# Where two small jobs stand in a Hawk/FoX decoder step: the first decay rows, and one key page of two

## The chip, the cores and the metric

The kernel runs on one core of a Trainium2 chip. The metric is the device time of one execution in microseconds; of several executions the median counts.

## The reference

One layer of a hybrid decoder is computed for 512 prompt tokens and, with the same weights, for 8 sample sequences of one token each, which have 1024 cached tokens in pages of 128. Cut to what matters:

```python
z = h @ w_in                                   # h: normed, modulated x
xr, gr, q, k, v, fl, ga, gb = jnp.split(z, cuts, axis=-1)
ya = (rg_lru(conv(xr)) * jax.nn.gelu(gr)) @ w_proj_a          # branch A
logf = jax.nn.log_sigmoid(fl + b_f)            # one per token and head
# prompt, 16 heads of 64, per head:
s = q @ k.T * scale + Fq[:, None] - Fk[None]   # F: cumulated logf
o = softmax(where(causal, s, -inf)) @ v
# samples: the same over cache_k[page_table], cache_v[page_table], cache_logf
yb = o @ w_proj_b
x = x + g1 * ((sigmoid(ga) * ya + sigmoid(gb) * yb) @ w_o)
x = x + g2 * ((silu(gu) * up) @ w_ffn_out)     # gu, up = norm(x) @ w_ffn_in
```

## The kernel before

All activations are kept transposed, 1024 features as 8 tiles of 128 partitions by 520 tokens (512 and 8). Every product with a weight matrix is taken one column tile of 128 at a time, in two halves of 260 tokens. To keep float32 accuracy weights and activations are split in a high and a low part: ScalarE casts the weight tile (`whi`, L246), VectorE subtracts (`wlo`, L248), and TensorE runs three matmuls for each of the 8 rows of tiles (`part_product`, L305). A half is thus 24 matmuls.

The part that the change touches is the stage from about 300 to 490 us. It runs key product 0 (`k_product`), value product 0, branch A's eight products `pa0` to `pa7` (`branch_a`), and then a loop of eight steps `i` over pairs of heads. "Step 0" below is the turn `i = 0`. A step runs the key product of the next pair, the value product of the next pair, and in between the attention of this pair and the scores of the next. `k_product(i + 1, mid_a)` and `v_product(i + 1, mid_b)` call `mid_a` and `mid_b` between their two halves. Names on the way:

- `decay_rows(i)`: for each of two heads SyncE loads a row of cumulated forget values to all partitions (`fb`), and GpSimd makes the masked forms `f0`, `fm` and `fb` of it by one copy and four additions. `scores` adds them to the scores.
- `scores(i, blocks)`: TensorE makes `sc` from `ksA`, `ksB` (keys) and `qqA`, `qlA` and so on (queries); VectorE adds the decay and takes the minimum (`mu`); ScalarE takes the exponential; VectorE takes the reciprocal of the sums; ScalarE and GpSimd scale. Blocks 0 and 1 are done in `mid_b`, blocks 2 and 3 behind the value product.
- `turn`: TensorE transposes the probabilities (`ptt`), ScalarE and VectorE split them (`ph`, `pl`). `values` multiplies them with the values (`po`).
- the cached pages: 64 key pages and 64 value pages of 512 KB share seven buffers (`pg`). GpSimd's queue loads pages up to a point in the program, SyncE's queue the rest. `key_page` loads a key page and puts it on the list `pend`. `key_sum` multiplies a page with the sample's query (L730) and reduces it (L731, into `S`), both on VectorE; then the buffer is free for the next page. A value page is multiplied on TensorE (`pv`, L817) and frees its buffer thus. When all pages of two samples are summed, `past_softmax` runs a chain of small steps (L768 to L797: `lgt`, `st`, `mk`, `pw`).
- `at(i, part)` in the loop starts page loads and value products by two tables, `KEYS_AT` and `VALUES_AT`. Steps 0 to 2 load two key pages each at part 2, within `mid_b`. Two are pending when the loop starts.

A scheduler puts the program of each engine in order by priority, which follows the order of the calls; `tc.issue_after(x)` keeps an instruction behind another in that order. Buffers in one heap (`slot`) rotate, so that the order of the calls also sets which buffer a tile gets. Every engine and every queue works in its order, and a DMA that waits holds up what is behind it in its queue.

Of the kernel before, what the change touches and what calls it, by code (L numbers as in the profile page):

```python
# [65 lines left out]
def kernel(ctx, tc, xT, par, gates, b_f, cst, cse, own, cache_k, cache_v, cache_lf, pt,  # L66
# [3 lines left out]
    pe, act, dve, pool, sp = nc.tensor, nc.scalar, nc.vector, nc.gpsimd, nc.sync  # L70
# [9 lines left out]
    def slot(name, cols=NT, dt=F32, parts=128):  # L80
        return heap.tile([parts, cols], dt, name=name, tag="slot")

    def bank(name, parts=128, cols=512):
        return psp.tile([parts, cols], F32, name=name, tag="bank")

    def small(name, parts, cols, bufs=4):
        return sm.tile([parts, cols], F32, name=name, tag="s_" + name, bufs=bufs)
# [71 lines left out]
    for jt in range(FF // 128):  # L159
# [5 lines left out]
        for name in BLOCKS:  # L165
            units.append((c, name, 4))
            if name in JOIN[jt]:
                g, i = JOIN[jt][name]
# [12 lines left out]
    state = {"n": 0, "dma": 0, "split": 0, "load": 22, "lead": 11, "due": 0, "age": 1}  # L181
    stores = []

    def store(dst, src):
        stores.append((dst, src))
# [4 lines left out]
    def flush():  # L190
        while stores:
            sp.dma_start(*stores.pop(0))
# [125 lines left out]
    def product(name, a, evac, mid=None):  # L318
        n = begin()
        for j in range(2):  # L320
            b = bank(f"{name}_{j}")
            half_product(n, j, a, b)
            evac(j, b[:, :HALF])
            if j == 0 and mid is not None:
                mid()
        run_later(n)

    def to(t, fn):
        def evac(j, b):
            t0, t1 = HALVES[j]  # L330
            fn(t[:, t0:t1], b)
        return evac
# [270 lines left out]
    ftd = drp.tile([H, NP], F32, name="ftd")  # L603
# [82 lines left out]
    pend = []  # L686
# [32 lines left out]
    def key_sum():  # L719
        _, s, j, pg, q, half = pend.pop(0)  # L720
        r = s // 2
        c = 256 * (r % 2) + 32 * j + H * (s % 2)
        with tc.issue_after(state["last"].ins):
            if half is not None:
                b, c = 8 * (r % 2) + j, H * (s % 2) + 8 * half
                dve.tensor_tensor(pg, pg, q.unsqueeze(1).to_broadcast([128, 2, 512]), ALU.mult)
                dve.tensor_reduce(S[r // 2].rearrange("p (b c) -> p b c", c=32)[:, b:b + 2, c:c + 8],
                                  pg.rearrange("p j (h d) -> p j h d", d=DH), AX.X, ALU.add)
            else:
                dve.tensor_tensor(pg, pg, q, ALU.mult)  # L730
                last = dve.tensor_reduce(S[r // 2][:, c:c + H], pg.rearrange("p (h d) -> p h d", d=DH), AX.X, ALU.add)  # L731
        summed[r] += 1
        if summed[r] == 2 * NPAGE:
            chains.append([9, past_softmax(r)])
        return None if half is not None else last
# [307 lines left out]
    def branch_a(i, mid=None):  # L1043
        product(f"pa{i}", g, to(tA[i], lambda t, b: dve.tensor_tensor(t, b, t, ALU.mult)), mid)
        store(tAd[i], tA[i])
# [93 lines left out]
    def q_load(i):  # L1139
        kvs[i]["qr"] = slot("qA", NP), slot("qB", NP)  # L1140
        for a, pr in enumerate(HEADS):
            for to_ in HEADS:
                sp.dma_start(kvs[i]["qr"][a][to_], qd[i, pr, :NP])

    def q_split(i):
        qq = slot("qqA", NP, F32R), slot("qqB", NP, F32R)
        ql = slot("qlA", NP, F32R), slot("qlB", NP, F32R)
        for a in range(2):
            t = kvs[i]["qr"][a]
            act.activation(qq[a], t, AF.Copy, scale=-(DH ** -0.5))  # L1150
            state["last"] = dve.scalar_tensor_tensor(ql[a], t, -(DH ** -0.5), qq[a].bitcast(F32), ALU.mult, ALU.subtract)
        del kvs[i]["qr"]
        kvs[i]["q"] = qq, ql

    def v_product(i, mid=None):
        t = slot("vt")
        product(f"v{i}", h, to(t, act.copy), mid)
        kvs[i]["vt"] = t
        pool.tensor_copy(v8[:, NS * i:NS * i + NS], t[:, NP:])
        store_now(vT[128 * i:128 * i + 128, :], t)  # L1160
# [17 lines left out]

    def decay_rows(i):
        for hd in (2 * i, 2 * i + 1):
            a = hd % 2
            if a == 0:
                f0 = slot("f0", 256)
            fb = slot("fb", 512)
            sp.dma_start(fb, ftd[hd:hd + 1, :].partition_broadcast(128))
            fm = slot("fm", 512)
            pool.tensor_copy(fm[:, :256], fb[:, :256])
            for dst, b in ((f0[:, 128 * a:128 * a + 128], 0), (fm[:, 384:], 1), (fm[:, 256:384], 2), (fb[:, 384:], 3)):  # L1190
                pool.tensor_tensor(dst, fb[:, 128 * b:128 * b + 128], msk, ALU.add)
            fmb = fm.rearrange("p (b c) -> p b c", b=4)
            fbs[hd] = f0[:, 128 * a:128 * a + 128], fmb[:, 0::3], fm[:, :384], fb

    def scores(i, blocks):
        ks = kvs[i]["k"]
        qq, ql = kvs[i]["q"]
        mus = small("mu", 128, 12, 4).rearrange("p (c b a) -> p c b a", c=3, b=2)
        for b in blocks:
            n = 128 * b  # L1200
            for a, pr in enumerate(HEADS):
                hd = 2 * i + a
                if b == 0:
                    prob[hd] = []
                    t3 = slot("p3", 512), slot("p02", 512), slot("p1", 256)
                    pts[hd] = (t3[1][:, :128], t3[2], t3[1][:, 128:], t3[0])
                sc = bank(f"sc{hd}_{b}")
                pe.matmul(sc[:, :n + 128], lhsT=qq[a][:, n:n + 128], rhs=ks[a][:, :n + 128], start=True, stop=False)
                pe.matmul(sc[:, :n + 128], lhsT=ql[a][:, n:n + 128], rhs=ks[a][:, :n + 128], start=False, stop=True)
                p = pts[hd][b]  # L1210
                mu = mus[:, :, b - blocks[0], a]
                ins = p[:, :n + 128], sc[:, :n + 128]
                if b == 1:
                    ins = [t.rearrange("p (b c) -> p b c", b=2) for t in ins]
                dve.tensor_tensor_reduce(ins[0], fbs[hd][b], ins[1], 1.0, 3.0e38, ALU.add, ALU.min, mu[:, 0:1])  # L1215
                act.activation(p[:, :n + 128], p[:, :n + 128], AF.Exp, bias=mu[:, 0:1], scale=-1.0, accum_out=mu[:, 1:2])  # L1216
                prob[hd].append((p, mu))
        dve.reciprocal(mus[:, 2], mus[:, 1])  # L1218
        for b in blocks:
            for a in range(2):  # L1220
                p, mu = prob[2 * i + a][b]
                (pool.tensor_scalar(p, p, mu[:, 2:3], None, ALU.mult) if a and i + 1 < KT else act.activation(p, p, AF.Copy, scale=mu[:, 2:3]))  # L1222
# [102 lines left out]

    k_product(0)
    q_load(0)
    decay_rows(0)
    v_product(0)
    for i in range(KT):  # L1330
        branch_a(i, (lambda: scores(0, (0, 1))) if i == KT - 1 else None)
        if i == 4:
            q_split(0)
            q_load(1)
    scores(0, (2, 3))
    g = None
    state.update(load=14, lead=8)
# [3 lines left out]
    def at(i, part):  # L1341
        tick(KEYS_AT[i][part], VALUES_AT[i][part])
        flush()

    for i in range(KT):
        last = i + 1 == KT

        def mid_a():
            v_tokens(i)
            if last:  # L1350
                turn(i, 0)
            at(i, 0)
            if last:
                with in_place():
                    join_weights()

        def mid_b():
            if not last:
                turn(i, 1)
            if not last:  # L1360
                scores(i + 1, (0, 1))
            at(i, 2)

        if not last:
            q_split(i + 1)
            decay_rows(i + 1)
        keys = None
        while pend:
            keys = key_sum()
            after[state["split"] + 2] = keys  # L1370
        if last:
            gate_b(6, mid_a)
        else:
            k_product(i + 1, mid_a, keys)
        turn(i, 1 if last else 0)
        at(i, 1)
        if i + 2 < KT:
            q_load(i + 2)
        (gate_b if last else v_product)(7 if last else i + 1, mid_b)
        values(i)  # L1380
        if last:
            spread_weights()
        if not last:
            scores(i + 1, (2, 3))
            at(i, 3)
        else:
            some_values(32)
        if i == KT - 4:
            sp.dma_start(em, cse)
        if i == KT - 2:  # L1390
            merge_load(0)
            state.update(load=22, lead=11)
# [344 lines left out]
```

## Time and profile before

| what | value |
|---|---|
| median of 3 runs | 1028.36 us (1027.15 to 1031.1) |
| profiled execution | 1033.71 us |
| its span | 1032.1 us |
| TensorE busy | 997.7 us, 97% of the span |
| VectorE busy | 793.5 us, 77% |
| ScalarE busy | 552.5 us, 54% |
| GpSimd busy | 330.7 us, 32% |
| HBM, read and written | 192.49 and 13.09 MB |

In the rows of the profile PE is TensorE, DVE VectorE, ACT ScalarE, POOL GpSimd and SP SyncE. In a timeline a row gives the start, the duration, the engine, the line, the operation, and output and input tiles; the bracket says how long the engine had been idle before it and what ended that. "PE pv L817 <- DMA pg" in the waits reads: TensorE's instruction that writes `pv` on line 817 waited for the load of a page. In the windows PEclk is the granted TensorE clock as a share of full speed, and the DMA share is that of the 16 engines' time.

### The profile page before, as it was taken

The page shows a single profiled execution, that of the slowest core. Times are in us where ns is not written, and L with a number is a line of the kernel's source. Part 1 is how long each engine was busy: PE and PEld are TensorE (multiplying, and loading weights), DVE is VectorE, ACT ScalarE, POOL GpSimd, SP SyncE. Part 2 cuts the span into 40 slices and gives each one's busy share as a digit, 9 for nine tenths or more (in the row PEclk, how much of TensorE's full clock was granted, in tenths as well). Part 3 has the DMA queues.
Part 4 walks back from the last instruction along what each step waited for, and adds up shares of the span by engine and source line. Part 5 has one row for each costly group of instructions (what it writes and reads, how often), then busy time and mean ns, then how long its engine had stood idle before and what let it go on. Part 6 is the DMA issues. An engine that isn't in the chain of part 4 may idle for free.

```text
span 1032.1 us, 21298 instructions
## 1 busy us (share of the span) xinstructions
PE 997.7 (97%) x7994; PEld 922.1 (89%) x7994; DVE 793.5 (77%) x1423; ACT 552.5 (54%) x1132; POOL 330.7 (32%) x424
## 2 busy tenths in 40 slices
PE   4999999999999999999999999999999999999996
PEld 1888989999898988878888989999999999999996
DVE  5446999998999977886756544778878888888864
ACT  4433665857682266776876223555444444445453
POOL 0214511111135134554430001485433423424212
PEclk9899999999999999999999999999999999999998
DMA  9888987878898998999665784323343342333212
GB/s 330 298 270 290 306 288 210 274 230 274 260 272 297 340 322 254 295 283 275 197 240 183 251 304 139 83 62 100 86 123 88 98 124 65 99 104 102 62 63 83
DMA packets 164378, 206.98 MB, mean 201 GB/s; under 512 B 9890, under 2 KB 125106, under 8 KB 164210
## 3 DMA queue, kind: packets, MB, share of 16 engines
q1 hardware_dynamic: 147554, 152.52, 47.7%
q0 software_dynamic: 13040, 46.67, 13.8%
q10 hardware_dynamic: 3680, 6.42, 1.7%
q8 instruction: 63, 1.03, 0.4%
q14 instruction: 41, 0.34, 0.1%
HBM read 192.49 MB, written 13.09 MB: 199 GB/s over the span
## 4 chain that ended last, share of the span: by engine, by line
PE 77%; DVE 10%; DMA 5%; ACT 4%; issue 3%; POOL 1%; SPq 0%; POOLq 0%; DVEq 0%; ACTq 0%
PE fo L305 12%; PE pb L305 4%; PE gb L305 4%; PE k L305 4%; PE v L305 3%; PE ga L305 3%; PE pa L305 3%; PE wo L305 3%; PE pv L817 2%; PE gr L305 2%; PE xr L305 2%; DMA wraw<-in_w_in_dram 2%; PE qp L527 2%; PE po L1265 2%; PE q L527 1%
## 5 line engine op out<-in xcount | busy, mean ns | idle before, releaser
L246 ACT CAST whi<-wraw 128x1024 fp32r<-128x1024 f32 (+1 forms) x79 | 82.1, 1040 | 135.2 <-PE pb L305 35.3
L248 DVE TENSOR_TENSOR wlo<-wraw,whi 128x1024 fp32r<-128x1024 f32 (+1 forms) x79 | 100.1, 1268 | 31.3 <-ACT whi L246 29.2
L270 ACT CAST wb<-ws 128x512 fp32r<-128x512 f32 x72 | 44.8, 622 | 92.2 <-PE fo L305 64.4
L305 PE MATMUL fo<-ach,wb 128*128 128x260 f32 x512 | 93.2, 282 | 0.0
L682 POOL DMA_DIRECT2D pg<-in_cache_k_dram x74 | 39.4, 533 | 141.8 <-DVE S L731 76.1
L305 PEld LDWEIGHTS fo<-ach,wb 128*128 128x128 f32 x512 | 78.9, 188 | 0.0
L271 DVE TENSOR_TENSOR wb<-wraw,wb 128x512 fp32r<-128x512 f32 x86 | 74.0, 860 | 6.0 <-ACT wb L270 5.0
L261 POOL TENSOR_TENSOR ws<-wraw 128x512 f32<-128x512 f32 x18 | 26.7, 1485 | 153.7 <-DMA wraw<-in_w_fi_dram 135.1
L270 ACT CAST wb<-wraw 128x512 fp32r<-128x512 f32 x86 | 53.4, 621 | 37.1 <-ACT cp L1625 6.2
L305 PE MATMUL fo<-acl,wb 128*128 128x260 f32 x256 | 72.3, 282 | 0.0
L271 DVE TENSOR_TENSOR wb<-ws,wb 128x512 fp32r<-128x512 f32 x72 | 59.9, 832 | 15.1 <-ACT wb L270 13.3
L730 DVE TENSOR_TENSOR pg<-pg,qb 128x1024 f32<-128x1024 f32 x48 | 58.4, 1236 | 1.3 <-DMA pg<-in_cache_k_dram 1.2
L731 DVE TENSOR_REDUCE S<-pg 128x16 f32<-128x1024 f32 x48 | 57.1, 1210 | 0.1
L1222 POOL TENSOR_SCALAR p<-p,mu 128x128 f32<-128x128 f32 (+3 forms) x28 | 35.6, 1282 | 51.6 <-DVE mu L1218 39.6
L305 PEld LDWEIGHTS fo<-acl,wb 128*128 128x128 f32 x256 | 48.2, 188 | 0.0
L1216 ACT ACTIVATE p<-p,mu 128x128 f32<-128x128 f32 (+3 forms) x64 | 35.3, 553 | 13.6 <-DVE mu L1215 13.3
L305 PE MATMUL v<-hh,whi 128*128 128x260 f32 x128 | 37.9, 296 | 0.6 <-DVE pl L1236 0.3
L305 PE MATMUL pb<-oh,whi 128*128 128x260 f32 x128 | 36.9, 288 | 1.0 <-ACT oh L1323 1.0
L305 PE MATMUL k<-hh,whi 128*128 128x260 f32 x128 | 37.3, 292 | 0.0
L817 PE MATMUL pv<-pg,pw 128*32 128x512 f32 x256 | 35.1, 604 | 2.0 <-DMA pg<-in_cache_v_dram 1.8
L305 PE MATMUL ga<-hh,wlo 128*128 128x260 f32 x128 | 36.3, 284 | 0.8 <-DVE wlo L248 0.8
L305 PE MATMUL gb<-hh,whi 128*128 128x260 f32 x128 | 37.0, 289 | 0.0
(1099 smaller groups left out, 3980.6 us busy)
## 6 DMA issues: line engine op xcount, KB each, us to landing
araw<-in_ada_w_dram SPq DMA_DIRECT2D x48, 512.0 KB, 6.9
wraw<-in_w_fi_dram SPq DMA_DIRECT2D x44, 512.0 KB, 4.1
pg<-in_cache_k_dram POOLq DMA_DIRECT2D x42, 512.0 KB, 6.2
pg<-in_cache_v_dram SPq DMA_DIRECT2D x42, 512.0 KB, 5.2
wraw<-in_w_in_dram SPq DMA_DIRECT2D x34, 512.0 KB, 7.3
wraw<-in_w_in_dram SPq DMA_DIRECT2D x11, 1024.0 KB, 10.4
pg<-in_cache_v_dram POOLq DMA_DIRECT2D x22, 512.0 KB, 6.6
pg<-in_cache_k_dram POOLq DMA_DIRECT2D x32, 256.0 KB, 5.9
```

Of the source, the lines that this page charges most:

```text
L246: state["act"] = act.copy(hi[:, :k1 - k0], src)
L248: state["last"] = dve.tensor_tensor(lo[:, :k1 - k0], src, hi[:, :k1 - k0].bitcast(F32), ALU.subtract)
L270: state["act"] = act.copy(t[:, :4], src)
L271: state["last"] = dve.tensor_tensor(t[:, 4:], src, t[:, :4].bitcast(F32), ALU.subtract)
L305: state["mm"] = pe.matmul(out[:, :t1 - t0], lhsT=wt[k], rhs=at, start=k == 0 and m == 0, stop=k == nk - 1 and m == 2)
L527: state["mm"] = pe.matmul(b[:, :HALF], lhsT=wt, rhs=at[:, t0:t1], start=k == 0 and m == 0, stop=k == 3 and m == 2)
L682: done.append(eng.dma_start(pg, cache[bass.ds(r, 1), :, c0:c1].rearrange("a p c -> (a p) c")))
L730: dve.tensor_tensor(pg, pg, q, ALU.mult)
L731: last = dve.tensor_reduce(S[r // 2][:, c:c + H], pg.rearrange("p (h d) -> p h d", d=DH), AX.X, ALU.add)
L817: pe.matmul(pv[0][32 * gq:32 * gq + 32, :], lhsT=pw[r][:, c:c + 32], rhs=pgs[gq // 2][:, 512 * hf:512 * hf + 512], start=j == 0, stop=j == ...
L1216: act.activation(p[:, :n + 128], p[:, :n + 128], AF.Exp, bias=mu[:, 0:1], scale=-1.0, accum_out=mu[:, 1:2])
L1222: (pool.tensor_scalar(p, p, mu[:, 2:3], None, ALU.mult) if a and i + 1 < KT else act.activation(p, p, AF.Copy, scale=mu[:, 2:3]))
```

## The change

Two jobs are put elsewhere; the number of instructions on each engine stays.

```diff
+    decay_raw = {}
+
+    def decay_load(i):
+        for hd in (2 * i, 2 * i + 1):
+            decay_raw[hd] = slot("fb", 512)
+            sp.dma_start(decay_raw[hd], ftd[hd:hd + 1, :].partition_broadcast(128))
+
     def decay_rows(i):
+        if 2 * i not in decay_raw:
+            decay_load(i)
         for hd in (2 * i, 2 * i + 1):
             a = hd % 2
             if a == 0:
                 f0 = slot("f0", 256)
-            fb = slot("fb", 512)
-            sp.dma_start(fb, ftd[hd:hd + 1, :].partition_broadcast(128))
+            fb = decay_raw.pop(hd)
             fm = slot("fm", 512)
...
-        dve.reciprocal(mus[:, 2], mus[:, 1])
+        state["sums"] = dve.reciprocal(mus[:, 2], mus[:, 1])
...
     k_product(0)
     q_load(0)
-    decay_rows(0)
+    decay_load(0)
     v_product(0)
     for i in range(KT):
+        if i == 2:
+            decay_rows(0)
         branch_a(i, (lambda: scores(0, (0, 1))) if i == KT - 1 else None)
...
             if not last:
                 scores(i + 1, (0, 1))
+            while pend:
+                with tc.issue_after(state["sums"].ins):
+                    key_sum()
             at(i, 2)
...
         keys = None
-        while pend:
+        if pend:
             keys = key_sum()
             after[state["split"] + 2] = keys
```

The GpSimd work of the first pair's decay rows is called before `pa2`; its two loads stay where they were. For every pair both loads now come ahead of the GpSimd work. Of the pending key pages only one is summed ahead of the key product of a step, the rest in `mid_b`, behind the reciprocal of the scores and ahead of the next page loads.

GpSimd between key product 0 and the pages that it loads, before (`qk` belongs to the key product, `v` to the value product):

```order
L1136 TENSOR_TENSOR qk_4420<-kt,q_573 128x8
L1189 COPY fm<-fb 128x256
L1191 TENSOR_TENSOR f_4516<-fb,cs 128x128
L1191 TENSOR_TENSOR fm<-fb,cs 128x128 x2
L1191 TENSOR_TENSOR fb<-fb,cs 128x128
L682 ISA
L682 DMA pg<-in_cache_k_dram 128x1024
```

and now:

```order
L1136 TENSOR_TENSOR qk_4420<-kt,q_573 128x8
L1159 COPY v_4421<-vt 128x8
L1199 TENSOR_TENSOR fb<-fb,cs 128x128
L682 ISA
L682 DMA pg<-in_cache_k_dram 128x1024
L682 ISA
L682 DMA pg<-in_cache_k_dram 128x1024
L682 ISA
L682 DMA pg<-in_cache_v_dram 128x1024
```

Before, the second head's five operations and the copy of `v` stood between these key pages and the first value pages. Now one addition of the ten operations is ahead of the pages; the nine others stand behind two more key pages.

VectorE in step 1, from the queries' split to the keys' split, before:

```order
L1151 SCALAR_TENSOR_TENSOR qlB<-qB,qqB 128x512
L730 TENSOR_TENSOR pg<-pg,qb 128x1024 x2
L731 TENSOR_REDUCE S<-pg 128x16 x2
L248 TENSOR_TENSOR wlo<-wraw,whi 128x1024
L1131 TENSOR_TENSOR ksA<-k_0_5816,ksA 64x260
```

and now, with the second page's place behind the reciprocal in two pieces:

```order
L1151 SCALAR_TENSOR_TENSOR qlB<-qB,qqB 128x512
L730 TENSOR_TENSOR pg<-pg,qb 128x1024
L731 TENSOR_REDUCE S<-pg 128x16
L1131 TENSOR_TENSOR ksA<-k_0_5814,ksA 64x260
L1131 TENSOR_TENSOR ksB<-k_0_5814,ksB 64x260
```

```order
L1226 RECIPROCAL mu<-mu 128x4
L730 TENSOR_TENSOR pg<-pg,qb 128x1024
L248 TENSOR_TENSOR wlo<-wraw,whi 128x1024
L731 TENSOR_REDUCE S<-pg 128x16
L1223 ISA p_6023,mu<-fm,sc_2_6134 128x384
```

One page's two operations have left the stretch ahead of `ksA` and stand ahead of the second half of the scores; `wlo` of the value product, which was ahead of `ksA`, follows the two key splits. In step 0 the second page likewise stands right behind the reciprocal. In step 3 the chain of the last two samples' softmax (L768, L770) starts half a step later.

SyncE's queue in step 1, around the pair's second value page (`pg_6178`), before:

```order
202 L682 DMA pg_6167<-in_cache_v_dram 128x1024 [waits DMAHW5_49,DMAHW4_49,PE_49]
203 L1143 DMA qA_5959<-qd_572 64x512 [waits DMAHW6_49]
204 L1143 DMA qA_5959<-qd_572 64x512 [waits DMAHW7_49]
205 L1143 DMA qB_5960<-qd_572 64x512 [waits DMAHW0_49]
206 L1143 DMA qB_5960<-qd_572 64x512 [waits DMAHW1_49]
207 L681 TENSOR_LOAD ptb_103
208 L681 ISA x2
209 L682 ISA
210 L682 DMA pg_6178<-in_cache_v_dram 128x1024 [waits DMAHW2_49,PE_49]
```

and now:

```order
213 L681 TENSOR_LOAD ptb_103
214 L681 ISA x2
215 L210 DMA wraw_6631<-in_w_in_dram 128x8x128 [waits DMAHW2_49,DVE_49]
216 L210 DMA wraw_6631<-in_w_in_dram 128x8x128 [waits DMAHW4_49]
217 L682 ISA
218 L682 DMA pg_6178<-in_cache_v_dram 128x1024 [waits DMAHW5_49,DVE_49]
219 L682 ISA
220 L682 DMA pg_6272<-in_cache_v_dram 128x1024 [waits DMAHW6_49,PE_49]
```

It waited for TensorE and stood ahead of the weights; now it waits for VectorE, for the sum of the second key page, whose buffer it gets, and stands behind them.

## The prediction

> **What bounds the kernel now.** I read the profile's page first, then TensorE's waits in the stage that the change touches, and then the chain and the timelines at the longest of them. The page:
>
> ```profile
> span 1032.1 us, 21298 instructions
> PE 997.7 (97%) x7994; PEld 922.1 (89%) x7994; DVE 793.5 (77%) x1423; ACT 552.5 (54%) x1132; POOL 330.7 (32%) x424
> ```
>
> TensorE is busy for 97% of the span and the change gives it the same matmuls. Time can only come from its idle stretches or from its clock. TensorE's waits between 295 and 565 us (total, times, longest):
>
> ```profile
> PE pv L817 <- DMA pg<-in_cache_v_dram: 1.8, 1, 1.8
> PE ptt L1231 <- ACT ph L1235: 1.3, 2, 0.7
> PE ptt L1231 <- DVE ksB L1131: 0.7, 1, 0.7
> PE sc L1208 <- DVE pl L1236: 0.6, 4, 0.2
> ```
>
> One wait is for a value page; the others lie where the transposed probabilities (`ptt`) and scores (`sc`) wait for VectorE or for ScalarE behind it. Busy time and granted clock of TensorE in the four places, and in the stretch behind the second:
>
> ```profile
> core 0: us, PE busy (x), PEclk, DMA share, GB/s
> 330.00:333.00 3.00, 1.16 (x11) 1.00 0.99 386
> 381.00:386.60 5.60, 3.60 (x26) 1.00 0.98 363
> 455.00:460.00 5.00, 3.83 (x28) 1.00 1.04 370
> 480.00:484.30 4.30, 4.04 (x33) 1.00 0.92 307
> 386.80:390.30 3.50, 3.50 (x18) 0.51 0.98 178
> ```
>
> Idle: 1.84 us in branch A's product, 2.00 in step 0, 1.17 in step 3, 0.26 in step 4. Each restart costs a little more. In the first place matmul starts stand 2.12 us apart (rows below) where pa's stand 0.12 apart: 2.00 lost for 1.84 idle, so 0.16 per restart. With about five restarts in step 0, four in step 3 and two in step 4 (my count of the stops) the losses are an estimated 2.8, 1.8 and 0.6 us. The last row is the price behind step 0: the clock is halved for 3.5 us.
>
> **Part 1, GpSimd's decay rows.** GpSimd, ScalarE and TensorE before pa3 (branch A's fourth product), and the loads' time to landing between 300 and 340 us (the last row):
>
> ```profile
> 317.12 0.40 POOL L1189 COPY fm<-fb 128x256 f32<-128x256 f32 x1 [5.67 <-DMA fb<-ftd]
> 322.10 1.09 POOL L682 DMA_DIRECT2D pg<-in_cache_k_dram  x2
> 325.58 0.18 POOL L1159 COPY v<-vt 128x8 f32<-128x8 f32 x1
> 325.71 1.08 POOL L682 DMA_DIRECT2D pg<-in_cache_v_dram  x2
> 318.32 1.05 ACT L246 CAST whi<-wraw 128x1024 fp32r<-128x1024 f32 x1 [4.70 <-PE pa L305]
> 330.70 0.28 PE L305 MATMUL pa<-gl,whi 128*128 128x260 f32 x1
> 332.82 2.25 PE L817 MATMUL pv<-pg,pw 128*32 128x512 f32 x8 [1.84 <-DMA pg<-in_cache_v_dram]
> pg<-in_cache_v_dram POOLq DMA_DIRECT2D x4, 512.0 KB, 7.5
> ```
>
> The value pages are issued at 325.71 because all ten decay operations and the wait for fb (5.67 us, to 317.12) stand ahead; they land about 7 us later (median 7.5), and `pv` stands until 332.82. In the new order one decay addition stays ahead, which still waits for fb (to about 317.1), then two key and two value pages. Four issues of 0.54 us put the value pages at about 318.6 to 319.3; a free buffer may hold them a little. Landing is at about 326.8, 4 us before the product before them ends at 330.8. The wait goes whole, **-2.0 us**. Two moved things cost nothing: the nine other decay operations run behind the page issues, and their readers are scores(0), behind pa's last product; the copy of v is ahead of the pages now but waits only for ScalarE, which has 4.70 us of idle time there.
>
> **Part 2, step 0.** The chain there:
>
> ```profile
> 375.08 2.35 DVE pg L730 x2
> 377.43 0.07 DVE S L731
> 378.48 1.21 DVE S L731
> 379.69 0.53 DVE mk L791
> 380.22 1.14 DVE wlo L248
> 381.38 0.42 DVE ksA L1131
> 386.57 4.66 PE v L305 x24
> ```
>
> Two multiplications and two reductions stand ahead of `ksA`. One pair of them moves behind the reciprocal: 1.17 + 1.21, say **2.35 us** earlier. VectorE has room for it there:
>
> ```profile
> 393.71 0.68 DVE L1269 TENSOR_TENSOR ol<-po,oh 64x512 fp32r<-64x512 f32 x1 [4.36 <-ACT side L1268]
> ```
>
> 4.36 us of idle time hold 2.35 us. But this chain is released by loads, and the DMA engines are at 0.92 to 1.04 of their time in every window above. If the load doesn't move up with the 2.0 us of part 1, TensorE arrives earlier at a chain that doesn't. I take half: 2.35 - 1.0 = **-1.35 us**, with bounds of -0.35 (no move) and -2.35 (all of it). Left of the stall: 2.8 - 1.35 = 1.45 us.
>
> **The clock.** The 24 matmuls behind step 0 take 4.66 us; a like group in step 1:
>
> ```profile
> 411.42 2.98 PE v L305 x24
> ```
>
> The difference is 1.68 us. The windows above tell when: after a loss of 2.8 us in 5.6 the clock halved; after 1.8 us in 5 and after one gap of 2.0 it stayed at 1.00. With 1.45 us left I take it as not halving: **-1.7 us**; bounds 0 and -1.7. [...]
>
> **Part 3, steps 3 and 4.** Step 3's chain:
>
> ```profile
> 450.56 1.05 ACT whi L246
> 451.64 1.43 DVE wlo L248
> 453.07 0.89 DVE S L768 x2
> 453.98 0.63 DVE mk L770
> 454.62 0.42 DVE ksA L1131
> ```
>
> The softmax rows at L768 and L770 move half a step later, behind the scores, and one page goes too. What is late next is `wlo`, which waits for `whi`: `ksA` starts at 453.1, not 454.62, **-1.5 us** of 1.8. In step 4 the reduction `mk` (0.53 in step 0) leaves the chain: **-0.5 us**. The moved rows' results are needed a step later and more; should their cover fail, TensorE would pay at most the same 1.5.
>
> **Part 4, what the change adds.** In steps 1 and 2 the page sum stands behind the reciprocal, and the pair's second value page waits for its buffer. Step 1 now:
>
> ```profile
> 414.55 0.18 DVE L1218 RECIPROCAL mu<-mu 128x4 f32<-128x4 f32 x1 [1.04 <-ACT p L1216]
> 415.79 1.23 DVE L248 TENSOR_TENSOR wlo<-wraw,whi 128x1024 fp32r<-128x1024 f32 x1 [1.07 <-ACT whi L246]
> 423.05 1.06 PE L817 MATMUL pv<-pg,pw 128*32 128x512 f32 x8
> pg<-in_cache_v_dram SPq DMA_DIRECT2D x42, 512.0 KB, 5.2
> DMA to landing us min/median/max: 3.4/5.3/9.0
> ```
>
> From 414.73: multiplication 1.2, `wlo` 1.2, reduction 1.2, so the page is issued at about 418.4. Its `pv` is the second half of the row at 423.05, about 423.6: 5.2 us, against a median of 5.2 and a spread of 3.4 to 9.0 between 385 and 470 us. No wait for these pages is among TensorE's waits of before. Taken: 0.3 us in each of steps 1 and 2, **+0.6**; bounds 0 and 3.8 each. Step 0 has some 4 us more, since `wlo` is late there. Queued behind that wait on SyncE are the next value pages, which wait for `pv` anyway; q's rows and the weights go ahead. In steps 1 and 2 `wlo` and the second half of the scores are at most 1.3 us late (2.4 of work against 1.07 of idle time); no row of TensorE's waits names those probabilities, so they have slack now: 0, bound 1.3 each.
>
> GpSimd scales probabilities beside the moved multiplication:
>
> ```profile
> 422.91 4.67 POOL L1222 TENSOR_SCALAR p<-p,mu 128x384 f32<-128x384 f32 x2 [1.07 <-DVE mu L1218]
> ```
>
> Two of them take 4.67 us while VectorE multiplies. [...]
>
> **Sum.** -2.0 - 1.35 - 1.7 - 1.5 - 0.5 + 0.6 = **-6.45 us**. The profiled execution took 1033.71 us (span 1032.1 and 1.6 around it), 5.35 above the median of 1028.36; the terms are stalls of the same stages, so I subtract from both: 1027.3 there, and a median of **1021.9**.
>
> **Rivals.**
> 1. *Value pages become the wait (slower).* The page of each of steps 1, 2 and 3 lands late. For: it is issued in the last moment, and the maximum is 9.0. Against: the median. Being slower by over 0.5% (5.1 us) needs 5.1 + 6.45 + 0.6 = 12.2 us from three places, 4.1 each: 2.4 of waiting and one halved clock of 1.7. So it decides from a landing of 5.2 + 2.4 = 7.6 us on; at 9.0 it is 3 x (3.8 + 1.7) = 16.5 - 7.05 = +9.4, 1037.8 us. Chance 0.17.
> 2. *The clock drop stays*, being tied to something else than these stalls: -4.75, 1023.6 us. For: step 3 and the gap of 1.84 us had no drop. Against: it is the only one in the stage and stands right behind its worst place. Chance 0.14.
> 3. *The loads set step 0.* Nothing of part 1 is passed on: step 0 gives -0.35, 2.45 us of stall remain, and the clock halves: -2.0 - 0.35 - 1.5 - 0.5 + 0.6 = -3.75, 1024.6 us. For: DMA near 1.0. Chance 0.10.
> 4. *It does not do what it says*: loads, which set the pace of the stage, fill each gap that it clears: 0, 1028.4 us. For: the DMA shares. Against: each of the four places names another releaser. Chance 0.07.
>
> **How the numbers follow.** The forecast has 0.52. Its own range: -8.1 (all of step 0, no page wait) to -5.1, 1020.3 to 1023.3. A measurement tells 0.5% (5.1 us: 1023.2 and 1033.5) from no change. Faster: 0.50 of the forecast and a third of rival 2, 0.55. Slower: rival 1 and some scatter, 0.19. The rest, 0.26, is the same. The range leaves out rival 1 and the ends: from 1020.3 less 1.2 of scatter (1028.36 - 1027.15) to rival 4 and about 1.2 above, **1019.1 to 1029.6**.
>
> **What would show it.** Right: no `pv` wait within pa; the value pages issued near 319 us; `ksA` of step 0 with one `pg` and one `S` ahead; PEclk at 1.00 behind it; `ksA` of step 3 right behind `wlo`. Wrong: `pv` rows with a releaser in_cache_v in steps 1 to 3, a stall in step 0 of over 2 us, or a halved clock in a new place.

## The result and the profile after

The changed kernel takes 1026.15 us (median; 1022.38 to 1030.44) against 1029.12 us (1027.15 to 1032.38) of the kernel before beside it. The ratio is 0.9961, with a 95% interval of 0.9947 to 0.9974: some 4 us less (2.7 to 5.5; the two medians alone differ by 3.0). The median is inside the predicted range of 1019.1 to 1029.6 us, but the gain is under two thirds of the predicted 6.45 us, and by the text's own bound of 0.5% it is "the same", to which the prediction gave 0.26.

The page after, the same two lines as before:

```profile
span 1025.3 us, 21277 instructions
PE 994.1 (97%) x7994; PEld 921.1 (90%) x7994; DVE 792.7 (77%) x1423; ACT 553.3 (54%) x1132; POOL 331.4 (32%) x424
```

TensorE's waits in the stage (total, times, longest), all that there are:

```profile
PE pb L305 <- ACT oh L1331: 1.0, 1, 1.0
PE ptt L1239 <- ACT ph L1243: 0.7, 1, 0.7
PE v L305 <- ACT row L797: 0.5, 2, 0.3
PE sc L1216 <- DVE pl L1244: 0.5, 3, 0.2
PE v L305 <- DVE pl L1244: 0.3, 1, 0.3
```

The `pv` row of before is gone, and so is one of the two `ptt` waits on `ph` and nearly all of the one on `ksB`. The rows of `pb` (1.0) and `v` (0.3 and 0.3) stood in the profile of before too, where the prediction's list leaves them out; one wait of `v` for `row` is new. GpSimd and TensorE in branch A:

```profile
315.05 0.46 POOL L1199 TENSOR_TENSOR fb<-fb,cs 128x128 f32<-128x128 f32 x1 [1.46 <-DMA fb<-ftd]
315.69 1.20 POOL L682 DMA_DIRECT2D pg<-in_cache_k_dram  x2 [0.17 <-issue]
317.66 1.18 POOL L682 DMA_DIRECT2D pg<-in_cache_v_dram  x2 [0.78 <-PE pv L817]
329.00 1.07 PE L817 MATMUL pv<-pg,pw 128*32 128x512 f32 x8
```

One addition is ahead of the pages, the value pages go out 8.0 us earlier (the stage itself starts 1.9 us earlier, a matter of the program's start, see the end), held by a buffer for 0.78 us, and `pv` takes 1.07 us where it took 2.25. That shorter row is worth 1.1 us more, which the prediction had in its fence and did not read: the second page of the pair landed later still, and TensorE waited for it within the row (3.1 us in all).

Step 0 on ScalarE and VectorE:

```profile
368.82 0.63 ACT L1150 ACTIVATE qqA<-qA 128x512 fp32r<-128x512 f32 x1 [1.64 <-DMA tAd<-tA]
371.74 1.22 DVE L730 TENSOR_TENSOR pg<-pg,qb 128x1024 f32<-128x1024 f32 x1
373.39 1.22 DVE L731 TENSOR_REDUCE S<-pg 128x16 f32<-128x1024 f32 x1
374.52 1.22 DVE L248 TENSOR_TENSOR wlo<-wraw,whi 128x1024 fp32r<-128x1024 f32 x1
375.77 0.42 DVE L1131 TENSOR_TENSOR ksA<-k,ksA 64x260 fp32r<-64x260 f32 x1
```

One page stands ahead of `ksA`, as said. But the head of the chain, `qqA`, waits 1.64 us for the store of a `tA` (branch A's result, whose buffer it gets). It did so before too, which the prediction did not see:

```profile
372.17 0.63 ACT L1150 ACTIVATE qqA<-qA 128x512 fp32r<-128x512 f32 x1 [1.39 <-DMA tAd<-tA]
```

VectorE in step 3 now, where the rows of L768 and L770 stood between `wlo` and `ksA` before:

```profile
444.11 1.23 DVE L248 TENSOR_TENSOR wlo<-wraw,whi 128x1024 fp32r<-128x1024 f32 x1 [1.40 <-ACT whi L246]
445.37 0.42 DVE L1131 TENSOR_TENSOR ksA<-k,ksA 64x260 fp32r<-64x260 f32 x1
```

TensorE and its clock in step 0, at the end of step 4, and behind it:

```profile
376.00:381.00 5.00, 3.60 (x25) 1.00 0.95 353
470.70:475.10 4.40, 3.79 (x25) 1.00 1.06 387
475.20:478.70 3.50, 3.50 (x17) 0.51 1.04 327
```

Step 0 still idles 1.40 us. No halved clock follows there any more; one follows step 4 instead, which now idles 0.61 us where it idled 0.26.

### The profile page after: what moved, and what is told of

It reads as the page before. It is cut to its first block, busy times and chain, and to the rows that moved or that the text cites. A ratio compares the mean times of both kernels' runs of the same rounds, so it can differ in the third digit from the quotient of the medians.

```text
span 1025.3 us, 21277 instructions
## 1 busy us (share of the span) xinstructions
PE 994.1 (97%) x7994; PEld 921.1 (90%) x7994; DVE 792.7 (77%) x1423; ACT 553.3 (54%) x1132; POOL 331.4 (32%) x424
## 4 chain that ended last, share of the span: by engine, by line
PE 86%; DVE 6%; DMA 4%; ACT 1%; issue 1%; POOL 1%; SPq 0%; DVEq 0%; ACTq 0%; POOLq 0%
PE fo L305 12%; PE gr L305 5%; PE gb L305 5%; PE pa L305 5%; PE pb L305 4%; PE v L305 4%; PE k L305 4%; PE ga L305 4%; PE xr L305 3%; PE pv L817 3%; PE wo L305 3%; DMA wraw<-in_w_in_dram 2%; PE qp L527 2%; PE po L1273 2%; PE q L527 1%; PE ptt L1239 1%
## 5 line engine op out<-in xcount | busy, mean ns | idle before, releaser
L248 DVE TENSOR_TENSOR wlo<-wraw,whi 128x1024 fp32r<-128x1024 f32 (+1 forms) x79 | 100.4, 1272 | 22.9 <-ACT whi L246 20.1
L271 DVE TENSOR_TENSOR wb<-ws,wb 128x512 fp32r<-128x512 f32 x72 | 63.1, 876 | 15.3 <-ACT wb L270 13.4
L270 ACT CAST wb<-wraw 128x512 fp32r<-128x512 f32 x86 | 53.5, 622 | 37.7 <-ACT cp L1638 6.5
L1230 POOL TENSOR_SCALAR p<-p,mu 128x128 f32<-128x128 f32 (+3 forms) x28 | 38.7, 1391 | 52.2 <-DVE mu L1226 38.1
L305 PE MATMUL v<-hl,whi 128*128 128x260 f32 x128 | 37.0, 289 | 0.0
L305 PE MATMUL v<-hh,wlo 128*128 128x260 f32 x128 | 36.9, 288 | 0.0
```

The lines of the kernel that those rows point to most:

```text
L248: state["last"] = dve.tensor_tensor(lo[:, :k1 - k0], src, hi[:, :k1 - k0].bitcast(F32), ALU.subtract)
L270: state["act"] = act.copy(t[:, :4], src)
L271: state["last"] = dve.tensor_tensor(t[:, 4:], src, t[:, :4].bitcast(F32), ALU.subtract)
L305: state["mm"] = pe.matmul(out[:, :t1 - t0], lhsT=wt[k], rhs=at, start=k == 0 and m == 0, stop=k == nk - 1 and m == 2)
```

## The experiments

To compare executions that start at different times, I cut the stage at the first matmul of each product in TensorE's timeline. In the table "v0" is step 0 from its value product's first matmul to the first `po` (a step's value part takes 8.1 us where nothing waits; v0 was 8.8 at best), "k1" is step 1 from its key product's first matmul to its value product's, and so on; "all" is from key product 0 to the product `pb`. In microseconds, one profile each (pa reaches to k0 and holds scores 0), with the halved windows of the clock within the stage:

| kernel | pa | v0 | k1 | k2 | k3 | v3 | k4 | v4 | v5 | gb | all | halved |
|---|---|---|---|---|---|---|---|---|---|---|---|---|
| before | 56.2 | 13.0 | 9.5 | 9.5 | 9.4 | 10.4 | 10.1 | 8.9 | 8.1 | 17.0 | 256.2 | step 0 |
| before, again | 53.5 | 9.9 | 9.5 | 9.5 | 9.4 | 10.4 | 10.1 | 8.9 | 8.1 | 17.0 | 250.5 | none |
| changed | 53.1 | 10.8 | 9.7 | 9.5 | 9.4 | 8.1 | 9.6 | 11.8 | 8.8 | 17.3 | 251.5 | step 4 |
| changed, again | 53.1 | 8.8 | 9.5 | 9.5 | 9.4 | 8.3 | 9.6 | 10.4 | 8.8 | 17.3 | 248.0 | none |
| decay only | 53.1 | 11.3 | 9.5 | 9.5 | 9.4 | 9.8 | 10.1 | 8.1 | 8.1 | 17.2 | 250.2 | none |
| pages only | 53.1 | 8.8 | 11.9 | 9.5 | 10.8 | 8.1 | 9.6 | 9.9 | 8.8 | 20.1 | 254.1 | none |
| pages, other buffers | 55.2 | 8.8 | 9.5 | 9.5 | 9.5 | 8.3 | 9.9 | 10.0 | 8.8 | 17.3 | 250.1 | none |
| step 3 ahead | 53.1 | 8.8 | 9.5 | 9.5 | 9.4 | 12.9 | 10.1 | 8.1 | 8.1 | 17.2 | 250.2 | step 3 |
| all behind | 53.1 | 8.8 | 10.9 | 11.3 | 10.2 | 8.1 | 9.6 | 10.1 | 8.8 | 17.2 | 251.9 | none |
| step 0 behind | 53.1 | 8.8 | 10.3 | 9.5 | 9.4 | 8.3 | 9.6 | 11.8 | 8.8 | 17.2 | 250.3 | step 4 |
| tA by ScalarE | 53.1 | 8.8 | 9.5 | 9.5 | 9.5 | 8.4 | 9.6 | 11.8 | 8.8 | 17.2 | 249.5 | step 4 |
| chain a quarter later | 53.1 | 9.4 | 9.5 | 9.5 | 9.4 | 8.3 | 9.5 | 8.6 | 10.3 | 17.0 | 247.9 | none |
| chain half later | 53.1 | 9.5 | 9.5 | 9.5 | 9.4 | 8.3 | 9.4 | 9.1 | 10.9 | 17.8 | 249.8 | none |
| both edits | 53.1 | 8.8 | 9.5 | 9.5 | 9.5 | 8.4 | 9.6 | 8.9 | 10.3 | 17.0 | 247.8 | none |

My theory was a sum of stalls fixed by the order, with step 0 released by loads; the rivals were that loads set the pace of the whole stage, that value pages become the wait, and that the halved clock has another cause.

**Each half of the change alone.** The decay rows' move, with both pages ahead of the keys:

```diff
-            while pend:
-                with tc.issue_after(state["sums"].ins):
-                    key_sum()
...
-        if pend:
+        while pend:
             keys = key_sum()
```

> The decay rows moved as in the change, both key pages of a step summed ahead of the keys as before. Theory A (the four stalls of TensorE, each by its own size): the value-page wait in branch A's product goes, with the second page's wait inside the row of 2.25 us, 3.1 us in all; but step 0's chain is released by loads and stores that move up by half only, so its stall grows by 1 to 1.7 us over the 2.8 of before, and the halved clock behind it stays. Net -1.4 to -2.1 us. Rival B (loads set the pace of the stage): everything is given back in step 0, 0 us. Rival C (nothing lags): -3.1 us or more.

Measured: ratio 0.9988 (0.9967 to 1.0008), median 1027.13 us against 1029.45. That is from 3.4 us faster to 0.8 slower, too wide to choose between A, B and C. The profile has pa at 53.1, and `qqA` of step 0 waiting for the store:

```profile
366.91 0.63 ACT L1150 ACTIVATE qqA<-qA 128x512 fp32r<-128x512 f32 x1 [1.18 <-DMA tAd<-tA]
```

v0 is 11.3. That is more than the 9.9 in the second profile of before, but the same as in the first without its halved clock (13.0 - 1.7), where `qqA` waited too. So it is not shown that step 0 gives back a part of branch A's gain, as A had it. The halved clock that I expected to stay was not there.

The other half, with the decay rows as before:

```diff
-    decay_load(0)
+    decay_rows(0)
     v_product(0)
     for i in range(KT):
-        if i == 2:
-            decay_rows(0)
```

(and `decay_rows` itself as before, each head's load ahead of its work.)

> One key page of two summed behind the scores as in the change, the decay rows as before. Theory A: the pv wait of 1.8 us in branch A stays; step 0's stall falls from 2.8 to about 0.5 us (2.35 less, as no arrival ahead of the loads eats it), the halved clock behind it goes (-1.7), step 3 gives -2.3, step 4 costs +1.0, and a halved clock there +1.7 if it is tied to the chain that moved there: -5.3 without it, -3.6 with it. Rival B (loads set the pace): about -2.3, the step 3 term alone. If A holds, the sum of this run and the decay-only run is larger than the whole change's -4.0.

Measured: 1.0017 (1.0000 to 1.0034), 1030.80 us. This was a miss: neither -5 nor -2, but no gain, and perhaps a little slower. The profile has v0 at 8.8 and v3 at 8.1, so the page gains came, and three losses that I had not expected. The first two rows of TensorE's waits:

```profile
PE ptt L1231 <- ACT p L1222: 2.1, 1, 2.1
PE pv L817 <- DMA pg<-in_cache_v_dram: 1.6, 2, 1.4
```

and from the timelines of TensorE and VectorE the rows behind them:

```profile
394.51 1.05 PE L817 MATMUL pv<-pg,pw 128*32 128x512 f32 x4 [1.36 <-DMA pg<-in_cache_v_dram]
526.92 0.29 DVE L1215 CUSTOM_DVE_ANT_0 p<-f,sc 128x128 f32<-128x128 f32 x1 [2.47 <-DMA out_kT_dram<-kt]
```

The second value page is late in step 1 and in step 3 (k1 11.9, k3 10.8): rival 1 of the prediction, at work. And in the last step a probability tile `p` got the buffer of a `kt` whose store to memory had not landed. VectorE stood for 2.47 us, ScalarE behind it, and TensorE for 2.1 us (gb 20.1 instead of 17.2). That is an accident of the rotation of buffers, which the order of the calls sets.

**The same without the accident.** The page change, with the first pair's buffers taken as in the change:

```diff
     decay_load(0)
+    decay_rows(0)
     v_product(0)
     for i in range(KT):
-        if i == 2:
-            decay_rows(0)
```

> The page change alone once more, but with the first pair's buffers taken in the order of the change (both fb first), the first pair's GpSimd work called where it stood before. Theory A (the pages-only run lost 2.1 us and more at 535 us because a probability tile got a buffer whose store of the keys had not landed, an accident of the rotation): without that accident the segment gb falls from 20.1 to 17.2 us and the time by 3 us, to about 0.3% under before; what is left against the changed kernel (ratio 0.996) is the worth of the decay rows' move, 1 to 1.5 us. Rival (the move of the decay rows is worth the whole 4.6 us between the pages-only run and the changed kernel): ratio 1.000 or more again, with a pv wait in branch A.

Measured: 0.9975 (0.9963 to 0.9987), 1026.50 us, as A said, and gb is 17.3. Between the two kernels lie 4.3 us, of which gb shows 2.8 and the value pages of steps 1 and 3 another 3.7, less 2.1 that this profile lost in branch A. They differ in the order of the heap's tiles and of each pair's two loads alone. In this profile the wait in branch A is there, as the decay rows stand ahead of the value pages:

```profile
330.59 1.05 PE L817 MATMUL pv<-pg,pw 128*32 128x512 f32 x4 [0.80 <-DMA pg<-in_cache_v_dram]
331.87 1.05 PE L817 MATMUL pv<-pg,pw 128*32 128x512 f32 x4 [0.23 <-DMA pg<-in_cache_v_dram]
```

The same order gave no wait in the pages-only profile (pa 53.1). The pages are thus worth 0.25% (0.13 to 0.37), the decay rows the remaining 0.14% (0.9975 to 0.9961), close to the 0.12% of the decay-only kernel. The halves add up, but the intervals are as wide as the smaller of them: that the decay rows bring anything, the times alone do not show.

**Are the stalls the same in every execution?** Both kernels once more, without an edit.

> The kernel before, once more, for a second profile of it. Theory A (its stalls are fixed by the order): a pv wait of about 1.8 us in branch A's product, 2.0 us idle in step 0, 1.2 in step 3, a halved clock behind step 0. Rival (they hang on when loads land in this execution, and the halved windows on the phase of the clock's window): at least one of the four is absent, as in the pages-only run, where the decay rows stood as before and no pv wait showed in branch A.

Measured: 1026.84 us in the profiled execution, against 1033.71 in the profile that the prediction used. The value pages and `pv` in branch A, and step 0's head:

```profile
322.89 1.08 POOL L682 DMA_DIRECT2D pg<-in_cache_v_dram  x2
329.82 1.52 PE L817 MATMUL pv<-pg,pw 128*32 128x512 f32 x8
366.95 0.62 ACT L1150 ACTIVATE qqA<-qA 128x512 fp32r<-128x512 f32 x1
```

The pages went out 2.8 us earlier than in the first profile, with the same order (the stage began 1.1 us earlier). `pv` lost 0.45 us (1.52 against 1.07) instead of 3.1. v0 is 9.9 us, and no halved window follows. The rival holds: most of the loss in two of the four places, and the clock, were matters of that execution. Of the four places only steps 3 and 4 read the same in both profiles.

> The changed kernel, once more, for a second profile of it. Theory A: 2.0 us idle in step 0, the halved window at step 4's end. Rival (phase and landing times): step 0 anywhere from 0 to 2.2 us of stall, the halved window absent or elsewhere; what stays the same is that no pv wait shows in branch A and that step 4 loses 1.1 us or more.

Measured: 1022.87 us. v0 8.8, no halved window, no wait in branch A; step 4 at 10.4 us against 8.9 of before. Between the two second profiles, which have no halved window, lie 2.5 us (before rounding): pa -0.5, v0 -1.2, v3 -2.1, k4 -0.6, -0.3 in each of steps 1 and 2, and given back v4 +1.5, v5 +0.7, gb +0.2; the rest are 0.1 or less.

**Step 4.** Where the last chain goes:

> The change, but in step 3 both key pages are summed ahead of the keys, so that the last softmax chain begins where it did before. Theory A (that chain, moved to step 4, costs there what step 3 gains): against the changed kernel step 3 loses about 1.8 to 2.3 us, step 4 gains 1.0, and the halved clock of 3.4 us at 475 us is gone (-1.7): between -0.9 and +1.3, so that the ratio to before is 0.995 to 0.997. Rival (the halving is a matter of phase and not of that chain): +0.8 to +1.3, and the profile still shows a halved window somewhere between 370 and 500 us.

The edit sums both pages ahead in step 3 alone:

```diff
-        if pend:
+        while pend:
             keys = key_sum()
             after[state["split"] + 2] = keys
+            if i < 3:
+                break
```

Measured: 0.9978 (0.9958 to 0.9998), 1027.49 us: not better than the change. v4 falls to 8.1 and v5 to 8.1, so step 4's loss is the chain's; v3 rises to 12.9, with a halved window behind it:

```profile
452.70:456.20 3.50, 3.50 (x18) 0.51 0.10 35
```

So a halved window can stand behind step 3 as well; in the three other profiles with the chain there (before twice, decay only) none did. The rows of the changed kernel's second profile, VectorE's and then TensorE's, show the price in step 4, and the last one, of the first profile of before, what `dg` took the place of:

```profile
467.62 0.67 DVE L779 TENSOR_SCALAR dg<-cs,st 32x256 f32<-32x256 f32 x1
470.29 0.68 DVE L823 TENSOR_TENSOR dr<-pv,pvm 128x512 f32<-128x512 f32 x1
471.01 0.75 DVE L825 TENSOR_TENSOR dr<-dr 128x256 f32<-128x256 f32 x2
471.68 1.88 DVE L1244 TENSOR_TENSOR pl<-ptt,ph 128x512 fp32r<-128x512 f32 x3
```

```profile
471.46 0.69 PE L784 MATMUL lgm<-dg,cs 32*128 32x256 f32 x2
472.42 0.39 PE L305 MATMUL v<-hh,whi 128*128 128x260 f32 x1 [0.26 <-DVE pl L1244]
```

```profile
481.26 0.61 DVE L791 TENSOR_REDUCE mk<-pw 128x32 f32<-128x256 f32 x1
```

`dg`, a step of the moved chain, takes 0.67 us between the key splits. The reduction `mk`, 0.61 us, which stood in this stretch before, has left it, so VectorE is hardly relieved; counted from the value product's start, the `pl` rows come 0.35 us later than before. `dr` was there already. Behind the scores `lgm`'s matmuls, which used to run in another half step, take TensorE 0.69 us, and the product's second half then waits 0.26 us. Two kernels start the chain, or its second part, later:

```diff
-            chains.append([9, past_softmax(r)])
+            chains.append([9 if r < 3 else 0, past_softmax(r)])
```

> The change, with the last two samples' softmax chain started a quarter step later. Theory A (step 4 loses 1.5 us because dg, 0.68 us, stands between the key splits and lgm's two matmuls stand ahead of the value product there): dg now stands behind the key splits but ahead of dr, so step 4's segment v falls from 10.4 to about 9.2; lgm moves behind the scores; -1 us against the changed kernel, and no halved window at step 4. Rival (the same work has to be done somewhere on a full TensorE and VectorE): the loss moves to step 4's end or step 5, 0 us.

Measured: 0.9958 (0.9942 to 0.9975), 1024.62 us. v4 falls to 8.6 and no halved window is there; step 5's v rises to 10.3, as value products moved into it (its k falls from 9.4 to 8.3), and 0.7 us more go between the two steps. Of the 1.7 us that step 4 gains on the changed kernel's second profile some 0.4 are left at the end of step 5, and the whole stage is no shorter (247.9 against 248.0, with v0 at 9.4): the rival's outcome for the most part. In the times the gain is within the interval of the change.

```diff
-        if r == 2:
+        if r >= 2:
             yield False
```

> The change, with the part of that chain from lgt on half a step later. Theory A: dg stands right behind the probabilities' split in the second half of step 4, step 4's segment v falls to 8.3 us; the chain's later parts come a half step later, so the last value pages' products wait at the start or move to the end: -1.5 us if the end has room, +1 to +3 if pv waits for pw in step 5 or at the end. Rival: 0, the loss appears in step 5's segment.

Measured: 0.9977 (0.9964 to 0.9989), 1025.98 us. Half a step is too late: v4 is 9.1, but steps 5, 6 and gb lose about 2.5 us together against the changed kernel's second profile, the rival's outcome in part.

**Step 0 and the value pages.** The store of `tA` through ScalarE's queue:

```diff
-        store(tAd[i], tA[i])
+        store_now(tAd[i], tA[i])
```

> The change, with branch A's results tA stored through ScalarE's queue as soon as they are made, in place of SyncE's queue, where they stand behind weight loads. Theory A (step 0's chain is released by the landing of a tA store, whose buffer the split query qqA takes): qqA starts 1 us or more earlier against k1's product, step 0's stall of 2.2 us in the profile falls below 0.7, and the time falls by 1 to 2.2 us against the changed kernel: ratio to before 0.994 to 0.995. Rival B (all 16 DMA engines are full from 313 to 400 us, so the store lands late on any queue): no change in step 0. Rival C: ScalarE, waiting in its order for VectorE's tA and for the queue, holds up whi and stalls TensorE in branch A: slower by 1 us or more.

Measured: 0.9964 (0.9950 to 0.9978), 1024.52 us, no different from the change. `qqA` starts at 364.57 without a wait, and v0 is 8.8. So the store can be taken out of the chain, and C did not happen; but the changed kernel's second profile has 8.8 without this edit. Among the seven profiles that sum one page ahead in step 0 and keep the store on SyncE's queue, three have `qqA` waiting over 1.6 us and v0 at 9.4, 9.5 and 10.8; the other four, with waits of 0.4 us at most, have 8.8. So the late store costs 0.6 to 2.1 us in some executions, on average too little for these times to show.

```diff
-        if pend:
+        if pend and i:
             keys = key_sum()
```

> The change, and in step 0 the first key page too is summed behind the scores, so none stands ahead of the keys. Theory A (step 0's stall is this chain, released by the loads): the chain is 2.35 us shorter, step 0's stall of 0 to 2.2 us goes, the value page of step 0 comes 2.4 us later and may cost 0 to 2 us: -2 to 0 us against the changed kernel, and no gain where the profile shows no stall in step 0 to begin with. Rival (value pages): a pv wait of 1 to 2 us in step 1, no gain.

Measured: 0.9973 (0.9957 to 0.9989), 1025.40 us. v0 is 8.8, and k1 10.3, as the value page comes later: the rival. One page behind the scores fits in step 0, two cost what they bring.

```diff
-        if pend:
+        if False:
             keys = key_sum()
```

> The change doubled: in steps 0 to 3 both pages are summed behind the scores, none ahead of the keys. Theory A: step 0's stall of 2.2 us goes (-1.8 to -2.2); in steps 1 and 2 the second value page is issued 2.4 us later than in the changed kernel, where the row after it was reached 4.9 us after the issue, so TensorE waits about 2 us for it in each of steps 1, 2 and 3: +4 to +6, perhaps with a halved clock (+1.7 each). Net +2 to +7 against the changed kernel. Rival (value pages land fast enough, as they did in the changed kernel): -2 us against the changed kernel, no pv wait in the waits.

Measured: 0.9969 (0.9951 to 0.9988), 1027.00 us. The page wait is there, in steps 1, 2 and 3 (k1 10.9, k2 11.3, k3 10.2: together 4.0 us). TensorE in step 2:

```profile
415.68 1.05 PE L817 MATMUL pv<-pg,pw 128*32 128x512 f32 x4
417.56 1.05 PE L817 MATMUL pv<-pg,pw 128*32 128x512 f32 x4 [0.82 <-DMA pg<-in_cache_v_dram]
```

A has the mechanism and, at its lower price, the size of the page wait; step 0's gain (2.1 against the changed kernel's first profile) eats half, and in the times the kernel can't be told from the change (0.9961).

**Both further edits together**, the store by ScalarE and the chain a quarter step later.

> The change with both further edits: tA stored through ScalarE's queue, and the last softmax chain a quarter step later. Theory A (step 0's stall of 0 to 2.2 us is gone in every execution with the first, step 4's loss shrinks by 0.9 us with the second): stage from key product 0 to pb of about 247 us, ratio to before 0.994 to 0.9955, median 1.0 to 2 us under the changed kernel's. Rival (each was within the scatter of executions and the loads set the pace): ratio 0.996 to 0.9965, no different from the change alone.

Measured: 0.9957 (0.9940 to 0.9974), 1024.28 us. The stage takes 247.8 us, but the ratio says no more than that it beats the kernel before; against the change alone (0.9961) it can't be told apart.

## Why the prediction was right and wrong

The direction was right, and of the four places the three with the larger terms gained. The size was 6.45 us for a measured 4.0 (2.7 to 5.5). That the range held the result is in part luck: the terms for branch A and the clock were too large, the moved chain's cost was missing, and rival 3's number (-3.75), the nearest to the result, has step 0 and its clock as the second profiles do not show them. Of the text's own signs, those of being right came, but in the first profile so did two of being wrong: a halved clock in a new place, and about 2.1 us lost in step 0 (v0 10.8 against 8.8). By its own steps:

- *The frame of the sum failed.* "The terms are stalls of the same stages, so I subtract from both" took the stalls of one execution, which was 5.35 us above the median, off the median. The second profile of before shows that this execution was slow at the very places: 5.7 us of stage (256.2 against 250.5), of which 2.7 in branch A, 3.0 in step 0 with its halved clock. A stall of one profile that hangs on a landing time is worth its mean over executions, not its length.
- *Branch A, -2.0.* The place and the cause hold: it is 53.1 in every profile with the pages first. The size was 3.1 in the first pair of profiles, 0.5 in the second. The four profiles with the decay rows first (56.2, 53.5, 53.1, 55.2) are 1.4 longer on average, and the halves of the change say 1.2 to 1.4 us, neither clear of the scatter.
- *Step 0, -1.35 (-0.35 to -2.35).* It was -0.4 between the first profiles, without the clock, and -1.2 between the second. The reading of what releases this chain failed: the text took it for loads, but `qqA` waits for `tA`'s store, 1.39 us in the very profile that the text used, and 1.64 and 1.18 in the changed and the decay-only kernel. So these waits do not show that something failed to move up with TensorE; the store lands late in some executions, with and without the change. Taking half of 2.35 came out near by luck. (By the text's own bounds for this term the small end of the forecast is -5.45, not -5.1.)
- *The clock, -1.7.* The halved window behind step 0 went, but it had not been there in the second profile of before, and a halved window stood behind step 4 in three of the seven profiles in which a page is summed behind the scores in step 3 and the last chain is as in the change. The trace does not confirm that 2.8 us of loss was the point: it followed 0.61 us of idle time in step 4. Rival 2, the window that belongs to something else, was nearer, but the runs do not show what sets it (see the end). The term should have been near 0.
- *Step 3, -1.5.* It was -2.1, and -0.6 more in step 4's key part.
- *Step 4, -0.5.* This failed in sign: +1.5, and +0.7 in step 5. The text said that the moved rows' results are needed a step later and took their cost as nothing. It looked at who reads the results, not at the work: `mk` left the chain as forecast, but `dg` came into its place (0.67 us for 0.61), and `lgm` (0.69 us) and `row` had to be done on TensorE and ScalarE in another step, where TensorE had no time to spare.
- *GpSimd beside the moved multiplication.* The sum gives it nothing, and that held: VectorE took 1.19 to 1.21 us for the multiplication in steps 0 to 2, GpSimd's two small scalings beside it took 2.38 to 3.13 us where they had taken 1.50, and no wait of TensorE names them.
- *Value pages, +0.6.* 0.2 and 0 in the two profiles of the change, but 2.4 and 1.3 in the pages-only kernel and 4.0 with all pages behind. Rival 1 had the right mechanism and is close by: in the changed kernel the page of step 1 goes out at 410.90, and its product, the second half of the row at 415.79, starts at about 416.2, as the text worked it out (5.3 against 5.2 us).

```profile
409.67 1.21 DVE L731 TENSOR_REDUCE S<-pg 128x16 f32<-128x1024 f32 x1
410.90 0.36 SPq L682 DMA_DIRECT2D pg<-in_cache_v_dram  x1
415.79 1.06 PE L817 MATMUL pv<-pg,pw 128*32 128x512 f32 x8
```

```profile
pg<-in_cache_v_dram SPq DMA_DIRECT2D x17, 512.0 KB, 5.5
```

The last row, from the DMA issues between 390 and 445 us, is the median to landing.

## What to carry to other kernels

Take a second profile before a stall of some microseconds is put in a sum: what reads the same in both is what an edit of the order can bring, and the rest hangs on landing times. When an edit moves a chain, cost its instructions where they go, not only where they leave. And an order of calls that allocate from a rotating heap is an edit by itself: gb lost 2.8 us by it in the pages-only kernel.

## What the runs showed of the hardware

In the first profiles of the two kernels the clock is halved (granted clock 0.50) for 3.41 us or a multiple of it: for 10.24 us (21.61 to 31.85) and 6.83 us (24.70 to 31.52) at the start of the program, and for 3.41 us in the stage (from 386.83 before, from 475.26 after). The start of the program shows it best. The granted clock between 15 and 40 us (the figure behind the count), in the first profile of before:

```profile
15.00:40.00 25.00, 21.19 (x171) 0.80 1.07 369
```

and in the second of the changed kernel:

```profile
15.00:40.00 25.00, 19.52 (x179) 0.93 1.07 371
```

The other two profiles of these kernels have 0.86. That is three, two and one windows at half speed (0.20, 0.14 and 0.07 of 25 us, doubled), with the same program up to there. The window behind step 0 cost about half its length, 1.7 us (24 matmuls in 4.66 us there, in 2.98 in step 1). With three windows key product 0 starts at 300.8 us, with two at 299.7 (before, again) and 298.9 (changed): up to 1.9 us of scatter ahead of the stage, almost half of what this change brought. The windows are not all of it, as 0.8 us lie between the two starts with two windows. Without this the spans of the first pair of profiles would be read as a gain of 6.8 us, of which 1.9 lie ahead of the stage.

From the end of the slow start to the halved window in the stage both profiles have a whole number of 3.413 us: the kernel before 355.0 us (31.85 to 386.83), 104.0 times, the changed kernel 443.7 us (31.52 to 475.26), 130.0 times. As far as two profiles show it, the window in the stage keeps step with those at the start, which gives the expectations' word phase its numbers. What brings a halved window in one execution and not in the next, the runs do not show. The length of a stop alone does not tell it: in the 5 us ahead of these two windows TensorE's longest gaps are 0.71 us (step 0) and 0.26 us (step 4), while 1.84 us at once in branch A's product of before and 1.36 us in step 1 of the pages-only kernel had no halved window behind them.
